# Projections of a hybrid attention block: three value groups and one gate group moved into double groups with seven products

## The chip, the cores and the metric

The kernel runs on one core of a Trainium2 chip, as one program. The metric is the device time of one execution in microseconds (us), as the median of the runs. Engines are named as the profile names them: PE (matrix products; PEld its weight loads), DVE (vector), ACT (scalar, activations), POOL (GpSimd), SP (the queue that issues the weight loads).

## The reference

One layer of a streaming encoder on 256 rows (SEQ) of width 2048 (D_MODEL), all in fp32:

```python
h = rmsnorm(x, g_mix[i])
proj = h @ w_in[i]            # 2048 -> 3*1024 + 3*1024 + 2*2048 columns
q_sb, k_sb, v_sb, q_ca, k_ca, v_ca, gate_sb, gate_ca = jnp.split(proj, splits, axis=-1)
y_sb = stick_breaking_attention(q_sb, k_sb, v_sb)       # 8 heads of 128
y_ca = chunked_relpos_attention(q_ca, k_ca, v_ca, rel_bias[i])   # 8 heads of 128
merged = sigmoid(gate_sb) * (y_sb @ w_sb_out[i]) + sigmoid(gate_ca) * (y_ca @ w_ca_out[i])
x = x + merged @ w_mix_out[i]
...                            # SwiGLU of width 5632, a gated projection of p, final RMSNorm
```

The first mixer ("sb") weighs values with log-sigmoids summed backwards over the keys; the second ("ca") is a softmax with a clipped relative bias. Only the part up to `merged` is touched here.

## The kernel before

**Precision.** Each fp32 operand is split into a rounded high part and a remainder: ACT casts (line 246, `hi`), DVE subtracts (line 228, `lo`). A product of two such operands is three products on PE (`three`, lines 275 to 277: high x high, high x low, low x high). The normalised input lies transposed in the table T1 (16 depth blocks x high/low x 256 rows).

**Pieces.** A weight matrix goes through in pieces of 512 KB: one load on SP's queue, one cast, one subtraction, then PE. A `group` of kind "row" makes 512 output columns for both row tiles, 8 pieces of two depth blocks, 96 products of 512 columns. A "feat" group makes 256 columns transposed (queries and keys), 4 pieces of four depth blocks; its products are in lines 351 and 353.

**Units.** A `unit` makes two row groups at once. Of its 8 pairs of depth blocks those in PAIRS (2, 4, 6) are done in a form with 7 block products instead of 8 (`split_pair`, `pair_products`), from sums of weight blocks (`xf`, DVE and ACT) and sums of table blocks (`pair_sums`, `sums_of`, kept in FP and `room`). Four of the seven products gather in sums of their own (`su`), which take two buffers of accumulator memory of 1024 columns, the same two that attention uses for its scores and results (`aux`, pool `ps_at`). After the last such pair `mid` adds the sums into the slots (one ACT copy, four DVE additions, lines 821 and 823), and `add_sums` adds the plain part (line 827).

**Order of the work.** The program text gives an order; a planner orders the instructions of each engine anew by the times it expects, with the text's order as priority. Attention of four heads is a list of six tasks (s1, s2, s3 for two heads, then for the other two: scores and their elementwise work; weights; weighted values). `push_attention` appends them to a queue, `flush(every)` issues one task per `every` pieces. Before a unit's first pair all waiting tasks are issued, because the `su` buffers follow.

The order before:

1. `w_ple_in` and the first value group (sb, heads 0 to 3), with the transposes and the norm of x between its pieces.
2. For each mixer and each half of its heads: a value row group, then four feat groups (queries, keys), one attention task per four pieces. For the first half the values are those of step 1; for the last half they come after the keys, and behind each of their pieces `scale_table` (line 771) multiplies two blocks of T1 by a power of two per row, which the units need.
3. Column 0 of both gates as two row groups, then three gate units (columns 1 to 3 of both gates).
4. The output projections, for each of four columns first sb, then ca; the post of each ca group merges both and makes a table of the result.
5. `w_mix_out` and everything behind it, not touched.

Values are scaled by the row norm on ACT (`scale_v`, line 550); gates get their sigmoid in `out_post` (line 848), whenever ACT has them ready. The gates share their room in memory with `ext`, the relative bias that is stored once to `ext_d` (line 607) and read back in skewed form for each two ca heads (line 718). `room`, the tile that holds sums in the units, shares its room with x, which is loaded again behind the last gate unit.

Of the kernel before, what the change touches and what calls it, by code (L numbers as in the profile page):

```python
# [9 lines left out]
F32 = mybir.dt.float32  # L10
# [6 lines left out]
P = 128  # L17
S = 256
# [25 lines left out]
def block_kernel(ctx: ExitStack, tc: tile.TileContext, x, p, w_in, w_sb_out, w_ca_out, w_mix_out,  # L44
# [118 lines left out]

    def unit(wsrc, n0s, kts, lhs, forms, ext, slots, mid, post, needs, row0=0, pairs=PAIRS, alone=False, after=None):
# [5 lines left out]
        g = dict(kind="unit", post=post, mid=mid, slots=slots, after=after, lhs=lhs, keep=None, forms=forms, ext=ext, pool=pool,  # L170
                 side=None if alone else 1 - pool)
# [110 lines left out]
    def pair_products(pc):  # L282
# [24 lines left out]
        if z:  # L307
            g["mid"](g)

    def products(pc):  # L310
# [48 lines left out]

    state = dict(loaded=0, split=0, at=0, raw=0, hl=0, ext=0, ps=ps_mm, fourth=None, ring=0, more=None)  # L360
    late = dict(ps=[ps_mm])
# [5 lines left out]
    def prefetch():  # L367
# [4 lines left out]
        while state["split"] < state["loaded"] and state["split"] <= state["at"] + 3:  # L372
# [10 lines left out]
            state["split"] += 1  # L383

    def later(fn, n=3):

        for _ in range(n):
            tasks.append((None, lambda: None))
        tasks.append((None, fn))

    def flush(every=1, until=None, in_turn=False):

        while state["at"] < len(pieces) and (until is None or until not in done):
# [71 lines left out]
    mid_stack = ExitStack()  # L465
    mp = mid_stack.enter_context(tc.tile_pool(name="mid", bufs=2))
    start = ExitStack()
# [76 lines left out]

    def v_tile():
        return mp.tile([P, NT, NB], F32, tag="v", name="v")

    def scale_v(v, ps):
        for t in range(NT):
            nc.scalar.activation(v[:, t, :], ps[t], AF.Identity, scale=rstd["mix"][:, t : t + 1])  # L550

    v0 = v_tile()
    stores = []

# [8 lines left out]
    def v0_post(ps):  # L563
        scale_v(v0, ps)
        with tc.issue_after(state["load"].ins):
            for store in stores:
                store()
# [84 lines left out]
    def weighted_values(v, h, kt, a0, a1):  # L652

        sh, sl = split_of(v[:, 0, h * P : (h + 2) * P], a0)
        yp = aux("yp")
# [116 lines left out]

    for mixer, make in ((0, sb_tasks), (1, ca_tasks)):
        for b in range(2):
            c0 = mixer * 3 * W + b * NB
            qT = mp.tile([P, 4, S], F32, tag="qT", name="qT")
            kT = mp.tile([P, 4, S], F32, tag="kT", name="kT")
            first = mixer == 0 and b == 0
            v = v0 if first else v_tile()
            end = mixer == 1 and b == 1  # L780
            if not first and not end:
                group("row", w2, c0 + 2 * W, range(KD), T1, lambda ps, v=v: scale_v(v, ps), needs=hneed)
            for dst, off, sc in ((qT, 0, SCALE), (kT, W, None)):
                for j in range(2):
                    then = None
                    if off and j == 1:
                        then = lambda t=make(qT, kT, v, 4 * b): push_attention(*t)
                    group("feat", w2, c0 + off + j * FB, range(KD), T1, feat_post(dst, 2 * j, sc, then), needs=hneed)
            if end:
                group("row", w2, c0 + 2 * W, range(KD), T1, lambda ps, v=v: scale_v(v, ps), needs=hneed,  # L790
                      after=lambda kts: scale_table(T1, kts))
            flush(4)

    def gate_post(m, c):
# [3 lines left out]
        return post  # L798


    room = bp.tile([P, 4096], F32R, tag="x", name="room")
    extra = {t: mp.tile([P, 1024], F32R, tag=u, name=t) for t, u in (("hi", "qT"), ("lo", "kT"))}
    work = mp.tile([P, 1024], F32, tag="v", name="work")
    state["fourth"] = extra.get
    state["work"] = lambda name: work[:, :512] if name == "af" else work[:, 512:]
    F_gate = [FP[:, 0], FP[:, 1], room[:, 3072:].rearrange("p (c f s) -> p c f s", c=2, f=4)]

# [20 lines left out]

    for m in range(2):
        group("row", w2, 6 * W + m * D, range(KD), T1, gate_post(m, 0), needs=hneed)  # L830
    flush(3)
    for i, pair in enumerate(PAIRS):
        pair_sums(T1, 2 * pair, F_gate[i])
    for c in range(1, 4):
        unit(w2, [6 * W + m * D + c * NB for m in range(2)], range(KD), T1, lambda kt: F_gate[kt // 4 - 1],
             [room[:, :3072]], lambda c=c: gate_slots(c), mid, add_sums, hneed, alone=True)
    flush(4)
    state["fourth"] = None
    x_ = bp.tile([P, NT, D], F32, tag="x", name="x")
    for c in range(4):  # L840
        dma_x.dma_start(x_[:, :, c * NB : (c + 1) * NB], xr[:, :, c * NB : (c + 1) * NB])

    def out_post(m, c):
        def post(ps):
            cs = slice(c * NB, (c + 1) * NB)
            gt = gates[:, :, m, cs]
            for t in range(NT):
                nc.scalar.activation(gt[:, t, :], gt[:, t, :], AF.Sigmoid, scale=r1["mix"][:, t : t + 1])
            for t in range(NT):
# [278 lines left out]
```

## Time and profile before

| | us |
|---|---|
| median of 3 runs | 1461.82 (1461.36 to 1461.98) |
| span of the profiled execution, first to last instruction | 1460.0 |
| PE busy | 1449.5 (99%) |
| PE's weight loads busy | 1213.5 (83%) |
| DVE busy | 1209.2 (83%) |
| ACT busy | 800.4 (55%) |
| stretch of queries and keys, heads 0 to 3 | 47.5 to 91 |
| stretch of the three gate units | 359 to 484 |

The profiled execution has no time of its own beside its span; the median of the runs is 1.8 us longer than that span. Rows of groups read: line, engine, operation, written tile <- read tiles, shape, count | total us, mean ns | idle time before them and what ended it. Matrix products are pipelined, so a product's own duration (0.39 us) is longer than the distance to the next.

### The profile page before, as it was taken

To read this page: it belongs to the slowest core of one execution; us is meant where nothing else is said; L and a number is where in the kernel's file an instruction comes from. 1 tells how busy PE (TensorE), PEld (TensorE's weight loads), DVE (VectorE), ACT (ScalarE), POOL (GpSimd) and SP (SyncE) were. 2 spreads that over 40 slices of the span, in tenths; PEclk is the share of its full clock that TensorE was granted. 3 is DMA by queue.
4 is the path that set the end of the run, shared out by engine and by line. 5 is a ranking of instruction groups with operands and counts; after the bars stand their busy time and mean duration, and the time that the engine had idled before them with its cause. 6 is when DMAs were issued, how large, how long until landed. Compare 5 with 4: busy or idle time off the path is not lost.

```text
span 1460.0 us, 18637 instructions
## 1 busy us (share of the span) xinstructions
PE 1449.5 (99%) x6867; PEld 1213.5 (83%) x6867; DVE 1209.2 (83%) x1524; ACT 800.4 (55%) x950; POOL 21.9 (1%) x44
## 2 busy tenths in 40 slices
PE   9999999999999999999999999999999999999997
PEld 7888888888888888888888888888888888888886
DVE  6666667796888667988999999999999989989775
ACT  6455555557555444555555555565645555556552
POOL 0100000000000000000000000000000000000000
PEclk9999999999999999999999999999999999999999
DMA  9855555565666766766666666666666666666772
GB/s 320 283 176 174 173 173 180 179 190 161 212 196 207 236 188 188 238 191 180 194 189 200 189 208 208 202 195 210 194 195 202 203 193 195 216 199 209 229 228 73
DMA packets 164733, 291.19 MB, mean 199 GB/s; under 512 B 9025, under 2 KB 42097, under 8 KB 164385
## 3 DMA queue, kind: packets, MB, share of 16 engines
q1 hardware_dynamic: 162528, 281.32, 61.9%
q0 software_dynamic: 2112, 8.68, 1.8%
q8 instruction: 54, 0.88, 0.2%
q14 instruction: 39, 0.31, 0.1%
HBM read 284.19 MB, written 5.77 MB: 199 GB/s over the span
## 4 chain that ended last, share of the span: by engine, by line
PE 99%; DMA 0%; DVE 0%; ACT 0%; SPq 0%; issue 0%; DVEq 0%
PE mm L276 24%; PE mm L277 24%; PE mm L275 24%; PE mm L351 8%; PE mm L353 4%; PE su L275 4%; PE su L276 4%; PE su L277 4%; PE tp L434 1%; DMA raw<-in_w_ple_in 0%; PE yp L659 0%; PE xps L488 0%; PE wt L750 0%; PE mml L277 0%; PE mml L276 0%; PE mml L275 0%
## 5 line engine op out<-in xcount | busy, mean ns | idle before, releaser
L228 DVE TENSOR_TENSOR lo<-raw,hi 128x1024 fp32r<-128x1024 f32 (+1 forms) x517 | 627.5, 1220 | 168.4 <-ACT hi L246 158.6
L246 ACT CAST hi<-raw 128x1024 fp32r<-128x1024 f32 (+1 forms) x399 | 418.1, 1051 | 427.9 <-PE mm L277 316.2
L276 PE MATMUL mm<-lo,T 128*128 128x512 f32 x1391 | 542.4, 390 | 0.0
L277 PE MATMUL mm<-hi,T 128*128 128x512 f32 x1391 | 538.9, 390 | 0.0
L275 PE MATMUL mm<-hi,T 128*128 128x512 f32 x1391 | 512.6, 391 | 0.0
L277 PEld LDWEIGHTS mm<-hi,T 128*128 128x128 f32 x1391 | 261.1, 188 | 53.8
L276 PEld LDWEIGHTS mm<-lo,T 128*128 128x128 f32 x1391 | 261.2, 188 | 53.4
L275 PEld LDWEIGHTS mm<-hi,T 128*128 128x128 f32 x1391 | 260.9, 188 | 53.6
L351 PE MATMUL mm<-T,hi 128*128 128x512 f32 x512 | 180.7, 399 | 0.0
L353 PE MATMUL mm<-T,lo 128*128 128x256 f32 x512 | 140.8, 280 | 0.0
L351 PEld LDWEIGHTS mm<-T,hi 128*128 128x128 f32 x512 | 95.4, 188 | 21.5
L264 ACT CAST hi<-raw 128x1024 fp32r<-128x1024 f32 x59 | 62.3, 1055 | 70.5 <-DVE raw L228 20.0
L353 PEld LDWEIGHTS mm<-T,lo 128*128 128x128 f32 x512 | 96.4, 189 | 1.2
L228 DVE TENSOR_TENSOR T<-xf,T 128x1536 fp32r<-128x1536 f32 x50 | 87.8, 1755 | 7.9 <-ACT T L267 7.9
L228 DVE TENSOR_TENSOR xf<-raw 128x512 f32<-128x512 f32 x118 | 80.9, 686 | 9.5 <-DMA raw<-in_w_in 4.9
L267 ACT CAST T<-xf 128x1536 fp32r<-128x1536 f32 x50 | 74.0, 1480 | 7.9 <-DVE xf L228 7.8
L261 ACT CAST hi<-raw 128x1024 fp32r<-128x1024 f32 x59 | 62.2, 1054 | 28.9 <-PE mm L277 22.8
L823 DVE TENSOR_TENSOR C<-su,C 128x512 f32<-128x512 f32 x72 | 47.7, 684 | 0.2
L827 DVE TENSOR_TENSOR C<-mm,C 128x512 f32<-128x512 f32 x72 | 46.9, 683 | 0.0
L228 DVE TENSOR_TENSOR xf<-raw,xf 128x512 f32<-128x512 f32 x59 | 40.4, 685 | 0.3
L228 DVE TENSOR_TENSOR raw<-raw 128x512 f32<-128x512 f32 x59 | 40.4, 685 | 0.1
L277 PE MATMUL mm<-T,T 128*128 128x512 f32 (+1 forms) x82 | 30.2, 368 | 0.0
(310 smaller groups left out, 1369.1 us busy)
## 6 DMA issues: line engine op xcount, KB each, us to landing
raw<-in_w_ffn_in SPq DMA_DIRECT2D x176, 512.0 KB, 3.9
raw<-in_w_in SPq DMA_DIRECT2D x160, 512.0 KB, 3.6
raw<-in_w_ffn_out SPq DMA_DIRECT2D x88, 512.0 KB, 4.6
raw<-in_w_mix_out SPq DMA_DIRECT2D x32, 512.0 KB, 4.7
raw<-in_w_ple_gate SPq DMA_DIRECT2D x32, 512.0 KB, 4.8
raw<-in_w_sb_out SPq DMA_DIRECT2D x16, 512.0 KB, 4.6
raw<-in_w_ca_out SPq DMA_DIRECT2D x16, 512.0 KB, 4.6
x<-in_x SPq DMA_DIRECT2D x4, 512.0 KB, 10.3
```

Source lines behind the costliest of these rows:

```text
L228: return nc.vector.tensor_tensor(out, a, b, ALU.subtract)
L246: state["cast"] = nc.scalar.copy(hi[:, c : c + m], raw[:, c : c + m])
L261: nc.scalar.copy(h1, raw1)
L264: nc.scalar.copy(h2, raw2)
L267: nc.scalar.copy(xh, xf)
L275: nc.tensor.matmul(ps, xh, hi, start=a, stop=False)
L276: nc.tensor.matmul(ps, xh, lo, start=False, stop=False)
L277: state["mm"] = nc.tensor.matmul(ps, xl, hi, start=False, stop=z)
L351: nc.tensor.matmul(ps, hi[:, i, f], lhs[:, kt, :, :].rearrange("p c s -> p (c s)"), start=a, stop=False)
L353: nc.tensor.matmul(ps[:, :S], lo[:, i, f], lhs[:, kt, 0, :], start=False, stop=z)
L823: nc.vector.tensor_tensor(C[i], q, C[j], ALU.add)
L827: nc.vector.tensor_tensor(g["C"][i], g["ps"][i], g["C"][i], ALU.add)
```

## The change

Two more units are made. The values of sb heads 4 to 7 go into a unit with column 0 of the sb gate; the two value groups of the ca mixer go into another one. Column 0 of the ca gate stays a row group, and comes right behind the first value group, with `scale_table` on its pieces; everything behind it uses the scaled table, and so `r1` in place of `rstd` (the rest of the row norm) in `scale_v`, in the broadcast `rbc` for queries and keys, and in the sigmoid of the gates.

The order is then: first values; ca gate column 0; queries and keys of sb heads 0 to 3 (the three `pair_sums` as tasks among them); the unit with the sb values 4 to 7; queries and keys of sb 4 to 7; queries and keys of ca 0 to 3; the unit of the ca values; three gate units; reload of x; queries and keys of ca 4 to 7; all four sb output projections; all four ca output projections. The alone-standing units get `hold`: attention tasks that wait are not issued from their first pair to `mid`. `flush` takes fractions, and `drain(6)` issues tasks until six are left. Tiles of the pool `mid` get one buffer for each half of the heads, in place of two in turn.

```diff
+    def unit(wsrc, n0s, kts, lhs, forms, ext, slots, mid, post, needs, row0=0, pairs=PAIRS, alone=False, after=None,
+             hold=False):
...
         if a:
-            while tasks:
+            while tasks and not g["hold"]:
                 run_task()
+            state["hold"] = g["hold"]
...
         if z:
             g["mid"](g)
+            state["hold"] = False
...
-            if tasks and state["at"] % every == 0:
+            n += 1
+            if tasks and not state["hold"] and int(n / every) > int((n - 1) / every):
...
-        broadcast(rbc, rstd["mix"], sp)
         halve_rstd("mix")
         broadcast(p2bc, p2, sp)
+        broadcast(rbc, r1["mix"], sp)
...
-    for mixer, make in ((0, sb_tasks), (1, ca_tasks)):
-        for b in range(2):
-            ...
-            if not first and not end:
-                group("row", w2, c0 + 2 * W, range(KD), T1, lambda ps, v=v: scale_v(v, ps), needs=hneed)
-            ...
-            if end:
-                group("row", w2, c0 + 2 * W, range(KD), T1, lambda ps, v=v: scale_v(v, ps), needs=hneed,
-                      after=lambda kts: scale_table(T1, kts))
-            flush(4)
+    def gate_unit(n0s, slots, post, hold):
+        unit(w2, n0s, range(KD), T1, lambda kt: F_gate[kt // 4 - 1], [room[:, :3072]], slots, mid, post, hneed,
+             alone=True, hold=hold)
+
+    group("row", w2, 6 * W + D, range(KD), T1, gate_post(1, 0), needs=hneed, after=lambda kts: scale_table(T1, kts))
+    flush()
...
+    for i, pair in enumerate(PAIRS):
+        tasks.append((None, lambda i=i, pair=pair: pair_sums(T1, 2 * pair, F_gate[i])))
+    queries_and_keys(0, 0, sb_tasks)
+    flush(4)
+
+    four_buffers(1)
+    gate_unit([columns(0, 1), 6 * W], lambda: value_slots((0, 1)) + [gates[:, t, 0, :NB] for t in range(NT)],
+              add_values((0, 1)), True)
+    flush(2)
+    state["fourth"] = None
+    queries_and_keys(0, 1, sb_tasks)
     flush(3)
+    drain(6)
+    queries_and_keys(1, 0, ca_tasks)
+    flush(2.67)
+    drain(6)
+
+    four_buffers(1)
+    gate_unit([columns(1, b) for b in range(2)], lambda: value_slots((1, 0)) + value_slots((1, 1)),
+              add_values((1, 0), (1, 1)), True)
     for c in range(1, 4):
-        unit(w2, [6 * W + m * D + c * NB for m in range(2)], range(KD), T1, lambda kt: F_gate[kt // 4 - 1],
-             [room[:, :3072]], lambda c=c: gate_slots(c), mid, add_sums, hneed, alone=True)
-    flush(4)
+        gate_unit([6 * W + m * D + c * NB for m in range(2)], lambda c=c: gate_slots(c), add_sums, True)
+    flush(1000)
     state["fourth"] = None
     x_ = bp.tile([P, NT, D], F32, tag="x", name="x")
     ...
+    queries_and_keys(1, 1, ca_tasks)
+    flush(2.67)
+    drain(6)
...
-    for c in range(4):
-        for m, wo in ((0, w_sb_out), (1, w_ca_out)):
-            group("row", wo[0], c * NB, range(8 * m, 8 * m + 8), T2, out_post(m, c),
-                  needs=lambda kt: ("y", kt))
-    flush()
+    for m, wo in ((0, w_sb_out), (1, w_ca_out)):
+        for c in range(4):
+            group("row", wo[0], c * NB, range(8 * m, 8 * m + 8), T2, out_post(m, c), needs=lambda kt: ("y", kt))
+        flush(2.67 if m == 0 else 1)
```

More of the change, by code (lines that the diff above doesn't have):

```diff
@@ L358, in group_products @@
             g["ps"] = None
-    state = dict(loaded=0, split=0, at=0, raw=0, hl=0, ext=0, ps=ps_mm, fourth=None, ring=0, more=None)
+    state = dict(loaded=0, split=0, at=0, raw=0, hl=0, ext=0, ps=ps_mm, fourth=None, ring=0, more=None, hold=False)
     late = dict(ps=[ps_mm])
@@ L383, in prefetch, with drain @@
             state["split"] += 1
+    def drain(left=0):
+        while len(tasks) > left:
+            run_task()
     def later(fn, n=3):
@@ L827, in add_sums, with four_buffers, columns @@
             nc.vector.tensor_tensor(g["C"][i], g["ps"][i], g["C"][i], ALU.add)
-    for m in range(2):
-        group("row", w2, 6 * W + m * D, range(KD), T1, gate_post(m, 0), needs=hneed)
-    flush(3)
-    for i, pair in enumerate(PAIRS):
-        pair_sums(T1, 2 * pair, F_gate[i])
+    def four_buffers(b):
+        more = {t: mp.tile([P, 1024], F32R, tag=f"{u}{b}", name=t) for t, u in (("hi", "qT"), ("lo", "kT"))}
+        state["fourth"] = more.get
+    def columns(mixer, b):
+        return mixer * 3 * W + 2 * W + b * NB
@@ new lines, in value_slots, with add_values, post @@
+    def value_slots(key):
+        v = values[key] = v_tile(key[1])
+        return [v[:, t, :] for t in range(NT)]
+    def add_values(*keys):
+        def post(g, b):
+            add_sums(g, b)
+            if b < len(keys):
+                scale_v(values[keys[b]], [values[keys[b]][:, t, :] for t in range(NT)], r1["mix"])
+        return post
+    def gate_unit(n0s, slots, post, hold):
+        unit(w2, n0s, range(KD), T1, lambda kt: F_gate[kt // 4 - 1], [room[:, :3072]], slots, mid, post, hneed,
+             alone=True, hold=hold)
```

54 lines of the change are left out of this document (26 added, 28 removed).

## The prediction

> **What bounds the kernel now.** I read the page first (busy shares, then the chain that ended last), then the waits of PE, then the chain in order of time for the pace of one product, and last the busy time by stretch.
>
> ```profile
> span 1460.0 us, 18637 instructions
> PE 1449.5 (99%) x6867; PEld 1213.5 (83%) x6867; DVE 1209.2 (83%) x1524; ACT 800.4 (55%) x950; POOL 21.9 (1%) x44
> ...
> PE 99%; DMA 0%; DVE 0%; ACT 0%; SPq 0%; issue 0%; DVEq 0%
> ```
>
> ```profile
> PE warm L532 <- POOL mhalf L99: 1.2, 1, 1.2
> PE mm L341 <- ACT hi L246: 0.5, 1, 0.5
> PE mm L276 <- DVE lo L228: 0.2, 1, 0.2
> ```
>
> ```profile
> 478.88 0.68 PE mm L275 x3
> ```
>
> The chain that ended last is PE from end to end, and the list of PE's waits is complete with three rows: 1.9 us in 1460, all at the start. So the order of the program, the casts on ACT, the subtractions on DVE and the loads all arrive in time; what PE has to issue sets the end. The row of the chain gives the pace: three 512-column products in 0.68 us, 0.227 us each.
>
> ```profile
> 47.50:91.00 43.50, 43.50 (x251) 37.94 (x252) 26.29 (x34) 20.17 (x27) 7.22 (x14) 1.00 0.77 249
> 286.60:322.00 35.40, 35.40 (x167) 29.58 (x166) 34.85 (x55) 19.26 (x31) 0.00 (x0) 1.00 0.63 188
> ...
> 401.00:442.50 41.50, 41.50 (x185) 34.37 (x184) 35.93 (x40) 23.65 (x24) 0.00 (x0) 1.00 0.65 203
> ```
>
> Columns after the stretch: its length, then busy us and count of PE, PEld, DVE, ACT, POOL, granted clock, DMA share, GB/s. The first row is the queries and keys of heads 0 to 3, the second the last value group with the scaling of the table, the third one whole gate unit. DVE, the next engine, is 26.29 of 43.50, 34.85 of 35.40 (98%) and 35.93 of 41.50 (87%) there, and PE waited in none of them. The clock is 1.00 throughout.
>
> **The change part by part.**
>
> *Products.* A row group of 512 columns is 16 depth blocks x 2 row tiles x 3 = 96 products; two of them are 192. A unit does the same two groups with 5 of its 8 depth pairs plain (5 x 24 = 120) and 3 in the seven-product form (3 x 21 = 63): 183. Three value groups and one gate group become two units (values of heads 4 to 7 with gate 0 column 0; both value groups of the second mixer), so 2 x 9 = 18 products go. At 0.227 us that is 4.09 us off PE. One gate group and the first value group stay plain; queries, keys, the three other gate units, attention, output projections and all behind them issue the same products.
>
> *DVE in a unit.*
>
> ```profile
> L228 DVE TENSOR_TENSOR lo<-raw,hi 128x1024 fp32r<-128x1024 f32 x17 | 20.8, 1221 | 2.1 <-ACT hi L246 1.4 <-ACT hi L264 0.6
> L228 DVE TENSOR_TENSOR room<-xf,room 128x1536 fp32r<-128x1536 f32 x3 | 5.3, 1758 | 3.4 <-ACT room L267 3.4
> L228 DVE TENSOR_TENSOR xf<-raw 128x512 f32<-128x512 f32 x6 | 4.1, 684 | 0.0
> L823 DVE TENSOR_TENSOR gates<-su,gates 128x512 f32<-128x512 f32 x4 | 2.7, 686 | 0.1
> L827 DVE TENSOR_TENSOR gates<-mm,gates 128x512 f32<-128x512 f32 x4 | 2.6, 682 | 0.0
> L228 DVE TENSOR_TENSOR raw<-raw 128x512 f32<-128x512 f32 x3 | 2.1, 685 | 0.0
> L228 DVE TENSOR_TENSOR xf<-raw,xf 128x512 f32<-128x512 f32 x3 | 2.1, 684 | 0.0
> ```
>
> These are all of DVE's groups in that gate unit (one of the 17 is a neighbour's). 16 x 1.221 + 5.3 + 4.1 + 2.7 + 2.7 + 2.1 + 2.1 = 38.5 us of durations, against 16 x 1.221 = 19.5 for two row groups: +19.0 for each of two units, so DVE goes from 1209 to about 1247. The records overlap a little, so the window counts 35.9. Covered by PE's 183 x 0.227 = 41.5 us as long as nothing else is put there: the gate units carry no attention now. The change keeps attention out while sums are open ("hold"), but not out of a unit's first four plain pieces.
>
> *Attention in the first new unit.* The first score task (s1) of heads 0 and 1 is issued right before that unit, s2 after two of its pieces, s3 after four, straight before the first seven-product piece.
>
> ```profile
> L682 DVE SCALAR_TENSOR_TENSOR ls<-zp,e 128x768 f32<-128x768 f32 x4 | 3.8, 958 | 3.0 <-ACT e L680 3.0
> ...
> L599 DVE TENSOR_TENSOR e<-e,past 128x256 f32<-128x256 f32 x8 | 3.0, 422 | 0.1
> ...
> L643 DVE TENSOR_TENSOR sl<-qT,sh 128x512 fp32r<-128x512 f32 x4 | 2.7, 687 | 0.2
> ...
> L643 DVE TENSOR_TENSOR sl<-kT,sh 128x256 fp32r<-128x256 f32 x4 | 1.7, 419 | 0.0
> ```
>
> The eleven groups of four head pairs (60 to 230 us) are four like the first, two like the second, three like the third, two like the fourth: 15.2 + 6.0 + 8.1 + 3.4 = 32.7, 8.2 us a pair. So this unit holds 35.9 + 8.2 = 44.1 us of DVE in 41.5 of PE. Bounds: 0 lost, if the queries and keys before it (26.29 of 43.50) take its first splits and those behind it take its last additions; 2.6 lost if nothing moves over, 5.2 by durations (38.5 + 8.2). I take 0, from the nearest row: 98% of DVE over 35.4 us with no wait of PE.
>
> *Scaling the table early.* It now rides on the first gate group, right behind the first value group.
>
> ```profile
> L771 DVE TENSOR_TENSOR T<-T,p2bc 128x512 fp32r<-128x512 f32 x32 | 20.6, 687 | 0.5 <-PE mm L276 0.3
> ```
>
> 16 of the 32 belong here: 16 x 0.687 + 8 x 1.221 = 20.8 us of DVE in 96 x 0.227 = 21.8. The same scaling cost PE nothing inside the 98% stretch, and the next group reads the last table blocks only in its fourth piece: 0. The three sums of table pairs (former lead-in of the units) go among the queries as tasks, where DVE has 17 us free.
>
> *First write of the gates.* They share their room with the bias table, so the new first gate group waits for that table's store.
>
> ```profile
> 46.45 1.26 ACT L550 ACTIVATE v<-mm,rstd_mix 128x512 f32<-128x512 f32 x2 [3.87 <-PE mm L277]
> 55.51 0.58 POOL L607 DMA_DIRECT2D ext_d<-ext  x1 [0.30 <-POOL ext L606]
> ext_d<-ext POOLq DMA_DIRECT2D x1, 1536.0 KB, 8.6
> ```
>
> The values end at 46.5, so the gates are copied out at 46.5 + 21.8 = 68.3; the store lands at 55.5 + 8.6 = 64.1. 4.2 us of room: 0. Were it later, ACT would stand with the casts queued behind that copy.
>
> *Other moves.* Weight loads keep their number (8 a row group, 16 a unit) and size on SP's queue. The reload of x on POOL's queue still follows the last gate unit, but the second mixer's eight bias loads now come behind it; their scores are wanted by attention alone, whose outputs are needed 45 us later. Attention of the last heads moves beside the first output projection: 16 x 1.221 + 2 x 8.2 (first mixer's price) + some 8 multiplications of 0.68 = 41.4 of DVE in 16 pieces x 12 x 0.227 = 43.6 of PE: tight, covered. Sum: 1460.0 - 4.1 = 1455.9 of span; the median of the runs stands 1.8 over the span, so 1461.8 - 4.1 = 1457.7.
>
> **The rivals.**
>
> *DVE becomes the bound in the first new unit.* For it: 44.1 in 41.5. Against: the 98% row. Price 2.6 (to 5.2): 1457.7 + 2.6 = 1460.3 (to 1462.9), within 0.2% (2.9 us, about what this kernel's measurement tells from no change).
>
> *The open sums wait for attention (ends slower).* The four sums take both auxiliary accumulator buffers, and the second of these is held by s3's result until DVE has copied it.
>
> ```profile
> 90.21 0.28 PE L648 MATMUL zp<-sh 128*128 128x256 f32 x1
> ...
> 118.22 0.68 DVE L626 TENSOR_TENSOR T<-yp,T 128x512 fp32r<-128x512 f32 x1
> ```
>
> ```profile
> 366.65 0.68 DVE L626 TENSOR_TENSOR T<-yp,T 128x512 fp32r<-128x512 f32 x1
> 370.37 0.39 PE L275 MATMUL su<-hi,T 128*128 128x512 f32 x1
> L848 ACT ACT_TABLE_LOAD x2 | 2.6, 1283 | 0.0
> ```
>
> At today's pace s1 to release takes 118.9 - 90.2 = 28.7 us. After the change the second buffer is wanted 48 + 12 products = 13.6 us behind s1. Of the 15.1 missing, PE can fill 3 + 24 products (the seventh product and the next two plain pieces), 6.1; and the sigmoid of the early gate costs a table load of 1.28 before s1's exponential. That leaves 10.3: 1468.0. It decides "slower" from 7.0 us unfilled on. Against: part of the 28.7 is spacing by issue, not latency; today's first unit also had s3 in its lead-in, released at 367.3, 3.0 ahead of the first sum, without a wait; and PE's order already threads attention between plain products.
>
> The Trainium skill ("ScalarE: Activation LUTs", What ACT_TABLE_LOAD costs) says that sigmoid and exp with ln lie in different sets and that each switch costs a load and a drain, 2.66 us together. The row shows 1.28 for the load and no drain of its own; by the page the rival would be 1469.4, an estimate.
>
> *Fewer products move nothing.* For it: PE's weight loads are busy only 83% of the span, as DVE is, so a "99%" could be pipelining and the end could hang elsewhere. Time then: 1461.8. Against: the pace row and the empty list of waits. The Trainium skill ("Perfetto Trace Analysis", Identifying the Most-Contended Engine) warns of just that: matmul busy time is no measure of headroom, weight-load busy time is. Here the waits decide against it.
>
> **How the numbers follow.** Forecast (4.1 off, at most 1.2 given back) 0.60; DVE bound 0.24; waiting sums 0.11; nothing moved 0.05. Faster 0.60, same 0.24 + 0.05 = 0.29, slower 0.11. Low end: 1457.7 less the 0.5 by which the lowest run lies under the median; high end: 1461.8, which takes in the DVE case up to 4.1 and the case of no effect. The forecast's own range is 1457.2 to 1458.9.
>
> **What would show it.** Right: PE with 18 products fewer, its list of waits still about 2 us, DVE near 1247 us, and stretches of unit 41.5 us long. DVE bound: waits of PE on lo of line 228 some 20 to 35 us into the first new unit (about 114 to 156 us). Waiting sums: one wait of PE of several us at the first su. A late bias store: ACT idle at the first gates copy near 68 us. The prediction is wrong if PE's waits grow by more than 1.2 us in all, or if the order planned anew costs PE switches between attention's products and the plain ones that the old order did not have.

## The result, and the profile after

The changed kernel takes 1474.77 us (median of 4 runs, 1473.51 to 1475.2), the kernel before beside it 1461.9: ratio 1.0086, 95% interval 1.0072 to 1.01. It is slower by 12.9 us where 4.1 us less was forecast. Its profiled execution has a span of 1472.7 us, 12.7 over that of before, so the profile shows the whole loss.

The page of the kernel after: span, busy time of the engines, the chain that ended last.

```profile
span 1472.7 us, 18664 instructions
...
PE 1452.7 (99%) x6849; PEld 1211.8 (82%) x6849; DVE 1242.6 (84%) x1570; ACT 820.4 (56%) x967; POOL 23.0 (2%) x44
...
PE 94%; ACT 2%; DVE 2%; DMA 1%; issue 1%; DVEq 0%; SPq 0%; ACTq 0%
```

PE issues 18 products fewer (6849 against 6867) and is still "99%" busy, but the chain that was PE from end to end now has 6% of others in it. What PE waited for (engine, line, releaser: us in all, times, longest):

```profile
PE mm L276 <- DVE v L818: 3.6, 1, 3.6
PE mm L276 <- ACT hi L247: 2.0, 2, 1.1
PE mm L354 <- ACT hi L247: 1.6, 2, 1.3
PE su L277 <- DVE room L229: 1.5, 2, 1.1
PE warm L541 <- POOL mhalf L99: 1.2, 1, 1.2
PE mm L344 <- ACT hi L247: 0.9, 1, 0.9
PE mm L277 <- DVE lo L229: 0.3, 2, 0.2
PE su L276 <- ACT room L268: 0.2, 1, 0.2
```

11.3 us in eight rows, against 1.9 us in three. (Most lines stand one or more below those of before: 228 is now 229, 275 is 276, 827 is 818.) To see where they lie I took, over all of PE's products, the distance to the next product's start less the pace of its kind (0.227 us for 512 columns of a row group), and summed this excess by stretch. It is 19.6 us in all before and 36.3 after, so 16.7 more; with the 4.1 us of the 18 products taken off, that is 12.6 of the 12.7 us. By place, before and after: 0 to 60 us 7.4 and 8.7 (7.1 to 8.7 in all runs here, so this is spread); 60 to 240 us, the first new unit and the queries and keys around it, 2.2 and 8.4; 240 to 450 us, the second new unit and the gate units, 2.6 and 8.8; the rest 7.4 and 10.3. (The growth in all does not depend on the paces taken; its share by place does, by 1 to 1.5 us, through the pace given to attention's small products.)

Busy time by stretch (length, then busy us and count of PE, PEld, DVE, ACT, POOL, granted clock, DMA share, GB/s): the first gate group with the scaling, the first new unit, the queries behind it, the second new unit in two parts.

```profile
47.50:70.00 22.50, 22.50 (x102) 18.41 (x101) 21.06 (x32) 11.45 (x14) 7.86 (x12) 1.00 0.80 265
115.00:160.00 45.00, 42.27 (x184) 32.66 (x183) 37.31 (x46) 28.55 (x31) 0.00 (x0) 1.00 0.52 155
160.00:205.00 45.00, 43.45 (x249) 37.47 (x248) 33.15 (x46) 28.66 (x36) 0.00 (x0) 1.00 0.56 177
255.00:300.00 45.00, 43.65 (x207) 35.59 (x206) 35.77 (x45) 26.57 (x31) 0.00 (x0) 1.00 0.56 172
300.00:345.00 45.00, 41.38 (x174) 33.39 (x173) 39.36 (x43) 26.00 (x26) 0.00 (x0) 0.96 0.63 196
```

The first row is clean: PE is full although DVE is 21.06 of 22.50. The units are not, and DVE is not simply full in them: it has 5.6 to 11.9 us to spare in each row in which PE stands.

**First place: attention in the lead of the unit.** In both new units the weighted values of two heads (`yp`) still stand right at the unit's first sums (`su`): 137.5 and 137.7 us in the first, 281.3 and 281.4 us in the second. Of the two `su` buffers the first gathers the sums with the weights `hi` and `lo`, the second those with the sums of weight blocks in `room`. The second unit, timeline of PE, and DVE's copy that releases `yp`'s buffer:

```profile
281.29 0.28 PE L657 MATMUL yp<-sh 128*128 128x256 f32 x1
281.40 0.40 PE L276 MATMUL su<-hi,T 128*128 128x512 f32 x1
...
293.40 0.39 PE L276 MATMUL su<-room,FP 128*128 128x512 f32 x1
...
294.54 0.39 PE L278 MATMUL su<-room,FP 128*128 128x512 f32 x1
...
298.29 0.50 PE L277 MATMUL su<-room,FP 128*128 128x512 f32 x1 [0.43 <-DVE room L229]
...
312.98 0.47 PE L276 MATMUL mm<-hi,T 128*128 128x512 f32 x1 [3.57 <-DVE v L818]
```

```profile
289.26 0.68 DVE L635 TENSOR_TENSOR T<-yp,T 128x512 fp32r<-128x512 f32 x1
```

No wait stands at the first `su` (281.40): the first buffer is free, and PE was given plain products to do beside it. The second buffer is released at 289.9 us and gets its first sum at 293.40. So the first pair's products now stretch from 281.4 to 294.5 us; in the fastest version below the same stretch is 268.1 to some 273. All that time they hold `room`, the one tile for the sums of weight blocks. ACT and DVE, which write it for the second pair, and both later:

```profile
294.96 1.49 ACT L268 CAST room<-xf 128x1536 fp32r<-128x1536 f32 x1 [0.30 <-PE su L278]
...
307.46 1.05 ACT L247 CAST hi<-raw 128x1024 fp32r<-128x1024 f32 x1 [1.99 <-DMA raw<-in_w_in]
```

```profile
296.48 1.76 DVE L229 TENSOR_TENSOR room<-xf,room 128x1536 fp32r<-128x1536 f32 x1 [0.56 <-ACT room L268]
...
308.55 1.23 DVE L229 TENSOR_TENSOR lo<-raw,hi 128x1024 fp32r<-128x1024 f32 x1 [1.20 <-ACT hi L247]
...
310.94 0.69 DVE L229 TENSOR_TENSOR xf<-raw 128x512 f32<-128x512 f32 x1 [0.56 <-DMA raw<-in_w_in]
...
312.15 0.68 DVE L818 TENSOR_TENSOR v<-mm,v 128x512 f32<-128x512 f32 x1
```

The cast starts right behind the product of 294.54, the subtraction behind the cast, and PE stands for them at the second pair (298.29). From there the unit is late, and at 309 PE waits 3.57 us for `add_sums` (line 818), whose additions free the accumulators. DVE takes its work in the planned order, and ahead of the addition that PE wants stand two of `mid`'s additions and two splits that wait for late weight loads: one stands 1.20 us for a cast which itself stood 1.99 us for its load (307.46, 308.55), the next 0.56 us for its own (310.94). The loads are late because the splits before them were: each of the seven loads issued from 295 to 310 us starts 0.03 us behind the DVE instruction that frees its raw tile, and lands 3.6 to 5.2 us later.

**Second place: table loads on ACT.** Groups of table loads between 45 and 480 us; before there were three in all (lines 848 and 737 of before).

```profile
L887 ACT ACT_TABLE_LOAD x4 | 5.1, 1283 | 0.1
L690 ACT ACT_TABLE_LOAD x4 | 5.1, 1283 | 0.1
L708 ACT ACT_TABLE_LOAD x4 | 5.1, 1283 | 0.1
L689 ACT ACT_TABLE_LOAD x1 | 1.3, 1283 | 0.0
L747 ACT ACT_TABLE_LOAD x1 | 1.3, 1283 | 0.0
```

14 instead of 3. The gates of column 0 are ready early now, and the planner put their sigmoids (line 887) between the attention's exponentials (689, 708) and logarithms (690), each of which then loads its own table. ACT just where PE waits for line 354:

```profile
167.28 1.28 ACT L887 ACT_TABLE_LOAD   x1
168.57 0.72 ACT L887 ACTIVATE gates<-gates,r_mix 128x512 f32<-128x512 f32 x1
169.32 1.28 ACT L690 ACT_TABLE_LOAD   x1
170.61 0.85 ACT L690 ACTIVATE e<-e 128x768 f32<-128x768 f32 x1
171.47 1.28 ACT L887 ACT_TABLE_LOAD   x1
172.77 0.72 ACT L887 ACTIVATE gates<-gates,r_mix 128x512 f32<-128x512 f32 x1
173.40 2.92 ACT L247 CAST hi<-raw 128x1024 fp32r<-128x1024 f32 x3
```

Six microseconds of table loads, sigmoids and one logarithm stand ahead of three casts, and the PE product that needs the first cast comes 1.5 us late.

### The profile page after: what moved, and what is told of

It is laid out like the page before. It is cut to its first block, busy times and chain, and to the rows that moved or that the text cites. A ratio compares the mean times of both kernels' runs of the same rounds, so it can differ in the third digit from the quotient of the medians.

```text
span 1472.7 us, 18664 instructions
## 1 busy us (share of the span) xinstructions
PE 1452.7 (99%) x6849; PEld 1211.8 (82%) x6849; DVE 1242.6 (84%) x1570; ACT 820.4 (56%) x967; POOL 23.0 (2%) x44
## 4 chain that ended last, share of the span: by engine, by line
PE 94%; ACT 2%; DVE 2%; DMA 1%; issue 1%; DVEq 0%; SPq 0%; ACTq 0%
PE mm L277 22%; PE mm L278 22%; PE mm L276 22%; PE mm L354 7%; PE su L277 4%; PE su L278 4%; PE su L276 4%; PE mm L356 4%; PE tp L443 1%; DVE lo L229 1%; ACT hi L247 1%; DMA raw<-in_w_in 1%; DMA raw<-in_w_ple_in 0%; PE mm L344 0%; DVE room L229 0%
## 5 line engine op out<-in xcount | busy, mean ns | idle before, releaser
L247 ACT CAST hi<-raw 128x1024 fp32r<-128x1024 f32 (+1 forms) x387 | 404.7, 1050 | 394.8 <-PE mm L278 294.7
L277 PE MATMUL mm<-lo,T 128*128 128x512 f32 x1349 | 527.0, 391 | 0.2 <-DVE lo L229 0.2
L278 PE MATMUL mm<-hi,T 128*128 128x512 f32 x1349 | 522.9, 390 | 0.0
L276 PE MATMUL mm<-hi,T 128*128 128x512 f32 x1349 | 498.7, 392 | 5.6 <-DVE v L818 3.6
L276 PEld LDWEIGHTS mm<-hi,T 128*128 128x128 f32 x1349 | 253.2, 188 | 59.3 <-issue 4.0
L277 PEld LDWEIGHTS mm<-lo,T 128*128 128x128 f32 x1349 | 253.7, 188 | 53.0 <-DVE lo L229 1.0
L278 PEld LDWEIGHTS mm<-hi,T 128*128 128x128 f32 x1349 | 253.7, 188 | 52.3
L265 ACT CAST hi<-raw 128x1024 fp32r<-128x1024 f32 x65 | 68.6, 1055 | 85.8 <-DVE raw L229 31.4
L229 DVE TENSOR_TENSOR xf<-raw 128x512 f32<-128x512 f32 x130 | 89.2, 686 | 8.9 <-DMA raw<-in_w_in 2.9
L262 ACT CAST hi<-raw 128x1024 fp32r<-128x1024 f32 x65 | 68.5, 1053 | 34.6 <-PE mm L278 28.6
L229 DVE TENSOR_TENSOR xf<-raw,xf 128x512 f32<-128x512 f32 x65 | 44.6, 686 | 0.4
L229 DVE TENSOR_TENSOR raw<-raw 128x512 f32<-128x512 f32 x65 | 44.5, 685 | 0.2
L229 DVE TENSOR_TENSOR room<-xf,room 128x1536 fp32r<-128x1536 f32 x15 | 26.4, 1757 | 11.2 <-ACT room L268 11.2
```

The lines of the kernel that those rows point to most:

```text
L229: return nc.vector.tensor_tensor(out, a, b, ALU.subtract)
L247: state["cast"] = nc.scalar.copy(hi[:, c : c + m], raw[:, c : c + m])
L262: nc.scalar.copy(h1, raw1)
L265: nc.scalar.copy(h2, raw2)
L276: nc.tensor.matmul(ps, xh, hi, start=a, stop=False)
L277: nc.tensor.matmul(ps, xh, lo, start=False, stop=False)
```

## The experiments

The theory after the result: the units themselves are as cheap as forecast; the loss is attention that no longer fits ahead of them, and the table loads make it worse. Rivals: the units cost more than they save (splits, late loads, DVE); the table loads are the whole loss; the values' unit is at fault. "Excess" is the sum described above: 60 to 240 us | 240 to 450 us. After has 8.4 | 8.8, before 2.2 | 2.6. Times stand against the kernel before on the same chip (1461.8 to 1462.1). A profiled execution's span lies 0 to 3 us under the median.

**Sigmoids late.** The sigmoids of the gates are issued behind the first mixer's last exponential.

```diff
-            nc.scalar.activation(ls, ls, AF.Exp)
+            state["sb_exp"] = nc.scalar.activation(ls, ls, AF.Exp)
...
+            with tc.issue_after(state["sb_exp"].ins):
                 for t in range(NT):
                     ...
                     nc.scalar.activation(gt[:, t, :], gt[:, t, :], AF.Sigmoid, scale=by["mix"][:, t : t + 1])
```

> The changed kernel with one edit: the sigmoids of the gates may only be issued on ACT behind the last exponential of the first mixer's attention. In the changed kernel they run from about 70 us on, and attention between 113 and 290 us shows 9 table loads (ln 4, exp 5) where the kernel before shows none. Table theory (each load makes ACT 1.28 us later than the order was planned for, and PE waits for late casts and late attention): the loads of the exp and ln lines vanish, PE's waits fall from 11.3 us to 2 to 4, time 1458 to 1463. Crowding theory (attention, held sums and seven-product splits together are too much for DVE in the first new unit and in the unit of the second mixer's values, whatever ACT does): loads vanish, but PE still waits 6 us or more, time 1468 to 1475.

1469.79 us, 1.0052 (1.0037 to 1.0067): 5.0 us less than the change, in the range of the crowding theory. Two table loads are left, excess 5.2 | 9.2. The stall of the queries at 173 us is gone; the second unit's is not.

**No attention in the first new unit.** Other spacing of the tasks (`flush`), none issued while the first unit runs.

```diff
-    flush(4)
+    flush(5)
...
-    flush(2)
+    flush(1000)
...
-    flush(3)
+    flush(2.67)
```

> The changed kernel with one edit: no attention task at all is issued before or inside the first new unit (heads 0 and 1 start behind it, six tasks more among the next queries and keys). The table loads stay. Crowding theory: the waits of PE between 114 and 175 us (about 7 us of excess) vanish, those in the unit of the second mixer's values stay; time about 1467 to 1469. Table theory: the waits move to where the attention now is; time 1471 to 1476.

1468.34 us, 1.0038 (1.0025 to 1.0051), excess 1.3 | 11.3. The first unit with nothing else in it costs no wait at all, although 12 table loads are left, so DVE does not bound it. The stall of the queries behind it is gone too. The attention put off meets the second unit, where PE's longest wait is now:

```profile
PE mm L276 <- DVE v L818: 4.2, 1, 4.2
```

**Table loads in the kernel before.** One tiny sigmoid behind the first values, so that exp and ln lose their common table there too.

```diff
+    early = const("early", [P, NT])
...
+        nc.scalar.activation(early, rstd["mix"], AF.Sigmoid)
```

> The kernel before with one added instruction: a sigmoid of a 128 x 2 tile into a scratch tile right behind the first values. It changes no result; it only makes ACT leave the common table of exp and ln, so that 11 table loads come into the first mixer's attention. Table theory: PE waits of several us appear between 90 and 240 us, time 1465 to 1475. If the loads matter only where DVE is crowded: PE waits below 1 us more, time 1461 to 1463, since DVE is at 53 to 77% in these stages.

1461.73 us against 1461.99, ratio 0.9998 (0.9989 to 1.0007): 10 table loads more (17 against 7 in the whole program), ACT busy 812.0 us in place of 800.4, and nothing lost. With the late sigmoids of the first experiment this says that the loads cost only where the attention is crowded against a unit.

**Both together.** The first two edits in one kernel.

> The changed kernel with both edits: sigmoids behind the last exponential of the first mixer, and no attention in the first new unit. If either theory holds, or both, PE's waits are near those of the kernel before (2 to 3 us) and the time is 1457 to 1460, the 4.1 us of 18 products under before. If waits of 5 us or more stay in the unit of the second mixer's values (292 to 315 us), a third cause is at work there (late loads of weights, which SP's queue shows), and the time is 1463 to 1468.

1472.64 us, 1.0065 (1.0048 to 1.0082), excess 1.4 | 14.9; all theories missed. The edit itself did it: a table load and four sigmoids in a row, 3.9 us of ACT, now came at 273.8 us in the lead of the second unit, and PE waited 3.8 us for the cast behind them. Work that is put behind one instruction lands wherever that instruction ends.

**Emptying the second unit by spacing**, with and without the first.

```diff
-    flush(2.67)
+    flush(2.5)
```

> The changed kernel with the first new unit empty of attention, and the tasks of each half of heads issued every 2.5 pieces in place of 2.67 during the next queries and keys, so that the sixth task comes at the 15th of 16 pieces and not behind the last. The table loads stay. Theory of the held sums (a result of attention in a unit's first plain pieces holds the second accumulator buffer; the sums of the first seven-product piece come late, its block of sums is released late, the next ones with it): nothing is held in either unit, PE's waits fall to 2 to 3 us, the half clock near 305 us does not come, time 1457 to 1459. Theory of the values (the unit of the second mixer's values stalls whatever runs beside it): waits of 4 to 6 us and the half clock stay there, time 1465 to 1468. Table theory: 5 us of waits somewhere between 150 and 300 us, time 1463 to 1467.

> The changed kernel with one edit: the six tasks of heads 4 to 7 of the first mixer come every 2.5 pieces, so that none falls into the unit of the second mixer's values. The first new unit keeps its attention. Held sums: the 8 to 9 us between 260 and 320 us go, the 7 us between 115 and 175 us stay; time 1464 to 1468. Theory of the values: nothing moves, 1473 to 1476.

1467.85 us, 1.004 (1.0026 to 1.0054), and 1473.88 us, 1.0082 (1.0068 to 1.0096); excess 1.3 | 12.1 and 8.5 | 8.3. In neither did the edit do what it was to do: the last `yp` before the second unit still starts at 277 and 280 us. Tasks issued earlier were not done earlier. The third pair of heads starts only when both pairs' keys are there (220.5 us in the second of these), and the fourth 29 to 31 us behind it. Their tiles `sh`, `sl`, `e` and `ls` have one buffer each; that this sets the distance was not tested.

**Gate units first.** The second experiment with the three gate units ahead of the ca values' unit.

> The changed kernel with the first new unit empty and the three gate units ahead of the unit of the second mixer's values; the last tasks of the first mixer still fall into the first of these four units, now a gate unit. Held sums: 8 to 11 us of waits in that gate unit (260 to 320 us), none in the values' unit; about the time of the kernel with the first unit empty, 1466 to 1470. Theory of the values: the wait moves to the values' unit, near 430 us.

1467.55 us in one run, excess 1.3 | 10.2.

```profile
PE mm L276 <- DVE gates L818: 3.9, 1, 3.9
```

The wait stays with whichever unit comes first behind the attention, now a gate unit. It is not the values' unit.

**Crowding the kernel before.** Its own first gate unit gets four attention tasks pushed against it.

```diff
-    flush(3)
+    flush(1000)
```

> The kernel before with one edit: no attention task beside the two gate groups of column 0, so that the four left over are issued in one go before the first seven-product piece of the first gate unit. Same work, same products. Held sums: the first gate unit now stalls as the two units of the changed kernel do, PE's waits 4 to 12 us near 365 to 400 us, time 1466 to 1475. If the stalls of the changed kernel come from its new groupings or value slots instead: no more than 2 us, 1461 to 1464.

1480.32 us, 1.0125 (1.0111 to 1.0139): 18 us lost without any new unit, more than expected. Excess 2.2 | 22.0, with 5.1 us of wait at an attention product, since the bunched tasks also wait for one another, and 4.2 us on line 827, the same addition. The collision alone, in the old order of projections, makes the same kind of wait.

**Tasks earlier.** `push_attention` takes one pair of heads; each pair's tasks are handed out as soon as its own keys are done, and none in the first unit.

```diff
+        t = make(qT, kT, (mixer, b), 4 * b)
...
-                if off and j == 1:
-                    then = lambda t=make(qT, kT, (mixer, b), 4 * b): push_attention(*t)
+                if off and mixer == 0:
+                    then = lambda j=j: push_attention(*t, hs=(2 * j,))
```

> The changed kernel with the first mixer's tasks issued earlier: those of two heads as soon as their own keys are there, every 2 pieces beside the first queries and keys, every 2.5 beside the next two; heads 0 and 1 still end inside the first new unit, the rest is done before the unit of the second mixer's values. The planned order of PE shows a result of attention between the first sums of the first unit and none in the other. Held sums: 5 to 8 us of waits in the first unit, none in the second (no half clock near 305 us); time 1462 to 1466. Theory of the values: 8 us stay between 260 and 320 us; 1470 or more.

1464.16 us, 1.0016 (1.0007 to 1.0026), excess 8.9 | 0.9, the time that the theory of held sums gave. The third pair starts at 208.9 in place of 221.9 us and the second unit is clean; the first pair's `yp` (134.1) still stands in the first.

**The gate group moved.** The ca gate's column 0 goes from the front to just ahead of the second unit (96 plain products to end attention beside); the scaling rides on the last keys of heads 0 to 3. Then, with late sigmoids and the scaling and sums spread:

```diff
-    group("row", w2, 6 * W + D, range(KD), T1, gate_post(1, 0), needs=hneed, after=lambda kts: scale_table(T1, kts))
...
-    queries_and_keys(0, 0, sb_tasks)
+    queries_and_keys(0, 0, sb_tasks, after=lambda kts: scale_table(T1, kts))
...
+    group("row", w2, 6 * W + D, range(KD), T1, gate_post(1, 0), needs=hneed)
+    flush(1000)
```

> The changed kernel, reordered: the plain group of gate column 0 of the second mixer stands behind the queries and keys of that mixer's heads 0 to 3, straight before the unit of its values, and so gives the last tasks of the first mixer 21.8 us of plain products to end in; the table is scaled behind the last keys of heads 0 to 3; the first new unit holds no attention but the first task behind its last sums. Products as in the changed kernel, one broadcast of 0.3 us more. The planned order of PE shows no attention inside either unit. Held sums: PE's waits as in the kernel before (2 to 3 us), no half clock before the end, and the 18 products show: 1457 to 1459. If 3 us or more of waits stay between 90 and 320 us, something else than held sums costs there, and the time is 1460 to 1468. Table theory: the loads are still there (sigmoid of the first gate column before the attention), so 1462 or more.

> Built on the run before (no attention inside either early seven-product unit), with its own two new waits taken away: the scaling of the last four blocks of the table and two of the three pair sums are spread over the first unit's lead instead of standing in one block ahead of it (3.8 us of wait on the pair sums there, and a half clock behind it), and the early sigmoids go behind the last exp of the attention (1.4 us and the table loads). Theory of the held second sum (products of a unit wait for attention's result): no wait over 1.5 us in either early unit, no half clock, 1457 to 1461 us, so at or below the kernel before, since the 18 products less are then all that is left. Rival, VectorE simply has too much to do at the start of the first unit wherever the pieces stand: 3 to 4 us of wait on the pair sums or on low parts stay there, 1462 to 1466 us. Rival, the values' unit itself costs more than it saves: its window shows over 3 us of wait with no attention in it, 1464 us or more.

1466.21 us, 1.0033 (1.002 to 1.0047), excess 10.6 | 0.4; and 1464.46 us, 1.0017 (1.0008 to 1.0026), excess 7.8 | 0.5. Neither unit shows a wait from its products, as the theory says, but my edit made a wait of its own, which the spreading did not take away:

```profile
PE mm L276 <- DVE sm L420: 3.8, 1, 3.8
```

Here the rival of a full DVE held: in the second of these kernels DVE works without a gap from 85 to 105 us, on the scaling, the sums and the splits at once.

**Tasks earlier and sigmoids late.** The two edits above in one.

> The change with its two-head attention tasks handed out earlier (as two runs before), and the early sigmoids behind the attention's last exp. If the 11 extra table loads cost only where attention is crowded against a unit, the stall of the next queries near 170 us and the half clock there go: about 3 us less than the 1464.2 us without it, 1460.5 to 1462. The first unit keeps its attention, so its about 4 us of stretched products and the 1.1 us wait on the block of sums stay. Rival, the loads were hidden already: 1463.5 to 1465, no change beyond the interval.

1462.65 us, 1.0004 (0.9995 to 1.0013), excess 3.9 | 2.4. The loads were worth 1.5 us here, half of what was expected. The wait of 1.1 us on `room` in the first unit stays.

**Pairs of heads in turn.** In addition the queries and keys of two heads come before those of the next two, so that the first pair starts about 11 us earlier (97.3 in place of 108.6), and the second pair is held until the first unit's sums are done.

```diff
-        for dst, off, sc in ((qT, 0, SCALE), (kT, W, None)):
-            for j in range(2):
+        for j in range(2):
+            for dst, off, sc in ((qT, 0, SCALE), (kT, W, None)):
...
+                    then = lambda j=j: (push_attention(*t, hs=(2 * j,)), state.update(hold=j > b))
```

> Built on the last run (tasks per two heads, handed out earlier, early sigmoids behind the attention's last exp, 1462.65 us): the queries and keys of the first two heads now come before those of the next two, so the first two heads' attention starts one group (about 14.5 us) earlier, and the second two heads' attention is held until the first unit's products are through. Theory of the held second sum: the first unit is then nearly free of attention and the second wholly (some 80 plain products lie between), so the first unit's stretch and its 1.2 us wait (about 1.9 us in all near 147 to 152 us) and the second's 0.9 us shrink to under 0.7 us together: 1458.5 to 1461 us, below the kernel before. Rival, the early units cost as much in other places as their 18 products save (VectorE full, splits late): no faster than 1461.5 us, with waits of PE on low parts taking over.

1458.51 us (10 runs, 1457.26 to 1459.84) against 1462.13: ratio 0.9975 (0.9966 to 0.9985). It beats both kernels. Excess 1.5 | 1.2. Its page, all its waits of PE, and the two stretches of the new units:

```profile
span 1456.7 us, 18659 instructions
...
PE 1445.4 (99%) x6849; PEld 1209.5 (83%) x6849; DVE 1241.5 (85%) x1570; ACT 805.6 (55%) x955; POOL 22.9 (2%) x44
```

```profile
PE warm L541 <- POOL mhalf L99: 1.2, 1, 1.2
PE mm L344 <- ACT hi L247: 0.9, 1, 0.9
PE mm L277 <- DVE lo L229: 0.5, 1, 0.5
```

```profile
115.00:160.00 45.00, 45.00 (x212) 37.63 (x211) 40.03 (x50) 24.83 (x29) 0.00 (x0) 1.00 0.59 189
...
300.00:345.00 45.00, 45.00 (x201) 37.24 (x200) 40.35 (x46) 26.88 (x29) 0.00 (x0) 1.00 0.64 199
```

With the same 18 products fewer PE is full in both, DVE does more in each stretch than in the change (40.03 against 37.31, 40.35 against 39.36), and every wait in a unit is gone. It is not that no attention is left there: in the first unit the first pair's `yp` (124.1 to 127.4 us) still stands at the first `su` (125.6), its buffer is released at 131.4, and the first pair's products stretch to 136.9 us. So a stretched first pair need not cost anything; it does when the next pair's work comes due before `room` is free, as at 298.29 us in the change.

**The first mixer's attention left out**, in the change and in the kernel before, by the same edit: its result is filled with the queries, so neither computes the reference's result.

```diff
         def s1(h):
-            ...
+            pass
+
+        s2 = s1
...
         def s3(h):
-            ...
+            split_y(qT[:, h : h + 2, :].rearrange("p k s -> p (k s)"), h0 + h)
```

> The change with the first mixer's attention left out of the computation (its products, exps and sums; its result is filled with the queries). Only the order of projections is left. To be read against the next run, the kernel before with the same left out. If all that was lost was attention against the two early units, this one is faster than that one by what the sum of the prediction gives for 18 products, 4.1 us, within 1 us. If the units cost more than they save in themselves (splits, sums, late loads), it is level or slower. Both near 1436 to 1442 us, as four pairs of heads with some 26 products each leave.

> The kernel before with the first mixer's attention left out in the same way, the partner of the run ahead of it: 4.1 us slower than that one if the 18 products are the whole difference once attention is gone, level with it or faster if the units cost more than they save in themselves.

1444.4 us (1444.27 to 1445.13) and 1448.31 us (1447.87 to 1448.58): the change is 3.9 us faster, though both times lie above the 1436 to 1442 us expected. All waits of PE, of the change and of before:

```profile
PE warm L541 <- POOL mhalf L99: 1.2, 1, 1.2
PE mm L344 <- ACT hi L247: 0.2, 1, 0.2
```

```profile
PE warm L532 <- POOL mhalf L99: 1.2, 1, 1.2
PE mm L341 <- ACT hi L246: 0.3, 1, 0.3
PE mm L276 <- DVE lo L228: 0.3, 1, 0.3
```

So the new order of projections saves what its products say, and nothing in the units eats it. Put differently, this attention adds 13.8 us to the kernel before (1462.1 - 1448.3) and 30.4 us to the change (1474.8 - 1444.4). The difference, 16.6 us, is the whole miss of the forecast (1474.8 - 1457.7 = 17.1) but for half a microsecond. The 11 extra table loads go with the attention here, so this pair does not part the two; the runs with late sigmoids do.

## Why the prediction was wrong, by its own steps

- *Products*: right. 18 fewer; forecast 4.09 us, 3.9 measured where nothing else differs.
- *DVE in a unit*: right. About 1247 us forecast, 1242.6 measured.
- *Scaling early, first write of the gates*: right at 0. PE is full from 47.5 to 70 us; a late bias store would have stood near 68.
- *Attention in the first new unit*: **this step failed.** It asked only whether DVE's busy time (44.1 us) fits into 41.5, and took 0. The runs showed in its place that the excess around this unit grew by 6.2 us (8.4 less 2.2), and fell to 1.3 with the unit emptied of attention; some 2.4 of it lies in the queries behind (160 to 180 us) and also goes with the table loads. What had to be asked was when each pair's chain of tasks ends against the unit's first sums. "98% of DVE with no wait" was no neighbour of it: that stretch held splits and the scaling, and no unit's sums whose buffers attention had to release first.
- *A step that was missing*: the second new unit, of which the prediction says nothing. Its sum could have been made from the trace of before: the first scores of the pairs start there at 90.2, 126.4, 163.5 and 199.7 us, so two pairs take 36.2 and then the 28.7 from scores to release, 65 us; between the keys of heads 4 to 7 and the second unit's first sums lie one stretch of queries and keys (43.5) and 48 plain products (10.9), 54 us. It does not fit. After the change the last two pairs start at 221.9 and 253.0 us, and the last release comes at 289.9, 8.5 us behind the unit's first sum (281.4). It cost another 6.2 us (8.8 less 2.6).
- *The sigmoid's table load*: counted as one load of 1.28 us. There were 11 more, since exp and ln parted as well. Ten such loads alone cost 0 (the early sigmoid in the kernel before); the 11 cost 5.0 us in the crowded places, and 1.5 us once the tasks are earlier. The Trainium skill ("ScalarE: Activation LUTs", What ACT_TABLE_LOAD costs) gives 1283 ns and a drain of about 1380 ns for each switch. The trace agrees on the 1283 ns; the next ACT instruction starts 0.01 us behind the load (168.57 behind 167.28 + 1.28), so no drain of its own shows here.
- *Other moves*: the excess behind 450 us grew from 7.4 to 10.3, and stays near 10 in every version of the change, the fastest too. The second mixer's attention moved there from the stretch before, and its excess, as it seems, with it. It was a move more than a cost: the pair without the first attention has 18.0 in all before and 17.8 after.

*The rivals.* "The open sums wait for attention" was the right mechanism at 0.11; its 1468.0 us, with 10.3 unfilled in one unit, lay 6.8 short. Its signature was not seen: no wait at the first `su`. From s1 to release it took 31.4 us (113.3 to 144.7), near the 28.7 assumed, but the unit's first sum came 24.4 us behind s1 and not 10.9, since the planner put plain products between. The wait came out one step further on, at `room` and at `add_sums`, in two units and not one. "DVE becomes the bound" is refuted for the change: 0.3 us of waits on line 229's `lo`, no wait at all in the first unit once it is emptied, and none in either unit of the fastest version, which does as much work on DVE; it does hold for the kernels with the scaling moved onto the last keys. "Fewer products move nothing" is refuted by the last pair. The prediction's own condition for being wrong (PE's waits grow by more than 1.2 us) came true with 9.4.

What is not settled: the way from the late release through `room` and the late loads to the addition at 312 us is read from the order of events in one trace; no run changed one link of it alone. Another buffer for `room` would be the direct trial of the first link, and it was not tried.

## What to carry to other kernels

Before a stage that takes over shared buffers is moved, add up the chains that must be through by then (their spacing and length, from the starts in the trace) and compare with the time left; busy shares of engines do not show this. Here the faster stage paid its products (3.9 of 4.1 us) once nothing collided, so when such a stage does not pay, leave the suspected neighbour out of both versions and compare. A stall that disappears at its named place may come out at the next single buffer.

## What the hardware showed that I had not expected

PE's granted clock fell to half behind waits. In the change the 3.57 us of wait at 309 us is followed by a stretch at half clock; columns as above.

```profile
310.60:314.00 3.40, 1.02 (x5) 0.87 (x6) 3.06 (x5) 0.72 (x1) 0.00 (x0) 1.00 0.63 213
314.00:317.41 3.41, 3.41 (x10) 2.60 (x9) 3.41 (x6) 0.41 (x1) 0.00 (x0) 0.50 0.49 139
```

The products there stand 0.43 us apart in place of 0.227, so the wait costs some 1.6 us more than its length. Apart from the last microseconds of every run, half-clock stretches in the other runs are 3.41, 6.83 or 10.24 us long, one, two or three times the same, behind waits of 3.4 to 5.1 us and once behind less. The Trainium skill ("TensorE: Matmul & The Clock Gate", Part 1: The HAM clock gate) describes a free-running window of about 3.4 us, after an idle one of which the clock is halved; the lengths agree. But a wait need not fill the window. In the change PE was busy for 1.02 of the 3.40 us before the clock fell. In the run with the tasks earlier the clock halved at 172.6 us behind waits of PE of 1.4 and 0.2 us, in a stretch where weight loads were busy 0.95 of 3.40 us.

```profile
169.20:172.60 3.40, 1.77 (x9) 0.95 (x7) 2.35 (x3) 3.39 (x5) 0.00 (x0) 1.00 0.00 0
172.60:176.01 3.41, 3.41 (x11) 2.94 (x12) 3.41 (x6) 1.68 (x2) 0.00 (x0) 0.50 0.54 165
```

And one wait of 3.3 us (the second unit emptied by spacing alone) was followed by none. How full a window must be was not measured.
